# A layer's mixers written as whole helpers with priority between projection units, instead of as interleaved streams of steps

## The chip, the cores and the metric

The kernel runs on one core of one Trainium2 chip. A core has TensorE (PE), VectorE (DVE), ScalarE (ACT), GpSimd (POOL) and SyncE (SP, which issues DMAs here), each with its own in-order queue of instructions, synchronised by semaphores. The metric is device time of one execution in microseconds; the time of a kernel is the median of its runs.

## What is computed

Two consecutive layers of a bidirectional encoder, on x of 2048 tokens by 1024 channels in float32. Each layer modulates its input with a scale and a shift from a conditioning vector, projects it, runs two mixers side by side, projects back and normalises:

```python
for l in range(DEPTH):                       # DEPTH = 2
    shift, scale, gate = jnp.split(mod[:, None, :], 3, axis=-1)
    h = x * (1.0 + scale) + shift
    if l % 2 == 0:  y = even_mixer(h, ...)   # neighbourhood attention || GLA
    else:           y = odd_mixer(h, ...)    # HGRN2 || Mamba-2 SSD
    x = layer_norm(DEEPNORM_ALPHA * x + gate * y, ln_g[l], ln_b[l])
```

The change is in the odd layer. Its mixer splits the projection into columns for HGRN2 (four heads of 128: cq, two forget gates cf_f and cf_b, ci, and the output gate cg) and for the state-space branch (its gate dz, 1024 channels dxbc, and dt). HGRN2 is a gated linear recurrence run in both directions; the state-space branch first filters dxbc along the sequence with four taps and SiLU, and then runs two chunked scans:

```python
oc = bidir_gated_recurrence(qc, bhld(ci, HGRN_HEADS), k_f, lf_f, k_b, lf_b)
yc = rms_norm(oc, hgrn_norm_g) ... * jax.nn.silu(cg)
xbc = lax.conv_general_dilated(dxbc, conv_w[:, None, :], ...)      # 4 taps
xs, bm, cm = split_cols(jax.nn.silu(xbc + conv_b), ...)
y = ssd_chunked(x_fw, a_fw, bm, cm) + rev(ssd_chunked(...)) + d_skip * xs
yd = rms_norm(y * jax.nn.silu(dz), ssm_norm_g)
return jnp.concatenate([yc, yd], axis=-1) @ w_out
```

## The kernel before, in words

**Projection.** A layer's input projection is cut into units (qf0 to qf3, ci0, ci1, b0, b1, x0 to x3, g0, g1, dz0, dz1 in the odd layer). Each unit has a weight that is loaded, split by ScalarE and GpSimd into a high and a low part (`wh`, `wl`, lines 185 and 186), and multiplied with the modulated input in high and low parts (`hH`, `hL`): three matmuls for each of eight slices of 128 channels (line 205). The sequence is done in two halves of 1024 tokens, half 1 first; a half has two groups of 512 tokens, g. `block` computes one tile of a unit and yields after every second slice, so a unit is a generator of steps. A finished tile is evacuated by ScalarE or VectorE and stored to DRAM by a DMA. `turn` is the change of halves: dz0 and dz1 of half 1 mixed with the building of half 0's input.

**HGRN2.** `Rec.pass_a(sg, ...)` (line 465) does one head on one stretch of 512 tokens (sg 0 to 3) in 12 steps: seven levels of a doubling scheme. A level multiplies `Q` and `Kp` by decay products `T` on VectorE (lines 532 and 534; line 536 is a third product on GpSimd), and has 16 small matmuls into a bank named `fine` (line 459), from which VectorE takes entries into `S` (line 497); the last level writes a bank `l` (line 522). Then come transposes `pk` (line 551), state updates `pu` (562) and output products `po` (580, 585). `pass_b` (line 608) is the second direction and the normalisation; `other(h, sg)` runs it for two heads.

**State-space branch.** `Ssd.steps` computes the step sizes and decays of one half, with five `sp` matmuls. `Ssd.conv` filters: a tile is 128 channels (i, 0 to 7) by 512 tokens (sg): load `cvx`, first tap on ScalarE (line 1152), three taps on VectorE (line 1154), sigmoid on ScalarE (1155), product on GpSimd (1156); for i under 6 four transposes `cvt` by TensorE (1165), a copy and a store. `cvx` and `cva` have two buffers. `Ssd.backward` (`back`) does one chunk of 128 tokens of the backward scan: load of `tk`, a GpSimd product (1203), two matmuls `pu` (1211) and the state step `sb` (1219, 1220). `local` and `forward` run later, beside the output projection.

**Order.** The program is not the order on the chip. A list scheduler simulates a time line with its own costs and issues, on each engine, what is ready, taking first what stands first in the program; `tc.high_priority(offset=2000)` counts an instruction as if it stood that much further ahead. In the kernel before, the odd layer's program order is itself fine: `woven(front, streams)` writes the steps of the units one by one, and after given numbers of them one step of a stream. HGRN2's chain (`lagging` mixes two stretches of a head half a pass apart) is one stream, in half 0 with `other` chained behind it; the steps, conv and back are another. A stream is given as (generator, first, per): it starts at front step `first`, and a step of it is written after every `per` front steps. `conv` is pipelined by one tile: `filtered` starts a tile, `put` transposes the one before. The even layer's attention has its own `weave`, which the change leaves.

What the odd layer's half 1 comes to in the program:

```python
woven(chained(steps_of("qf1 ci1 qf2 b1 qf3 x0 x1 x2 x3 g0 g1", 1), turn),
      (hgrn(range(4), 1), 0, 2), (chained(steps(1), conv(3), back(3)), 90, 8))
```

## Time and profile before

| what | value |
|---|---|
| time, median of 3 runs | 2748.59 us (2747.47 to 2750.7) |
| the profiled execution's own time | 2755.94 us |
| its span, first to last instruction | 2754.1 us |
| mean granted TensorE clock | 0.955 |
| busy: PE, DVE, ACT, POOL | 2526.8, 1493.4, 1122.9, 1326.1 us |

The profile is of one execution; its busy times and durations belong to that execution's time, which is not the median. A busy PE can still be slow: the granted clock says by how much, 1.00 being the full 2.4 GHz. The even layer and the beginning of the odd one, up to 1403.0 us of the span, are in both kernels the same instructions in the same order; the stages after it are cut at the first matmuls of ci0 (half 1), dz0 in the turn, ci0 (half 0), g1 (half 0), at the end of the last dz1 matmul, and at the first matmul of the output projection.

### The profile page before, as it was taken

Reading aid. Unit: us, or ns where it says so; the run is one execution under the profiler, and the core shown is the slowest. Engines: PE = TensorE matmul, PEld = TensorE weight load, DVE = VectorE, ACT = ScalarE, POOL = GpSimd, SP = SyncE. Lnnn points to the kernel's source line nnn. Section 1 sums busy time; section 2 is a strip of 40 time slices with the busy share of each in tenths; the row PEclk is TensorE's granted clock in tenths of the full one; section 3 lists DMA queues with packets and bytes.
Section 4 is the critical chain, followed back from the end, with each engine's and each line's share of the span. In section 5 each row is a group of like instructions: output and inputs, shape, how many; then the busy total and the mean of one; then the engine's idle time right before and its main releaser. Section 6 shows DMA issues by size and latency. Waiting matters only on the chain. (4 is left out here: it accounts for less than half of the span.)

```text
span 2754.1 us, 53110 instructions
## 1 busy us (share of the span) xinstructions
PE 2526.8 (92%) x20888; PEld 2125.2 (77%) x20888; DVE 1493.4 (54%) x2493; ACT 1122.9 (41%) x2355; POOL 1326.1 (48%) x1305
## 2 busy tenths in 40 slices
PE   7999999999999799998999999999999888788987
PEld 5877778887778677877788777888877677566776
DVE  6223335124433676765626356432625788687895
ACT  3152323244343644543323444232424453554652
POOL 4252325244442544434535556335534677575874
PEclk9999999999999899999999999999999999798998
DMA  8525434323365878775553335434436567543331
GB/s 275 159 99 169 145 115 132 115 95 106 109 221 181 253 210 234 202 205 167 173 201 126 106 124 177 136 127 131 134 105 207 169 200 235 182 148 112 117 115 62
DMA packets 269800, 432.46 MB, mean 157 GB/s; under 512 B 25936, under 2 KB 143600, under 8 KB 269552
## 3 DMA queue, kind: packets, MB, share of 16 engines
q1 hardware_dynamic: 267248, 420.69, 48.7%
q0 software_dynamic: 2304, 8.39, 0.8%
q8 instruction: 165, 2.70, 0.4%
q14 instruction: 83, 0.68, 0.1%
HBM read 296.60 MB, written 132.38 MB: 156 GB/s over the span
## 5 line engine op out<-in xcount | busy, mean ns | idle before, releaser
L186 POOL TENSOR_TENSOR wl<-wraw,wh 128x1024 fp32r<-128x1024 f32 (+2 forms) x116 | 290.5, 2524 | 293.9 <-ACT wh L185 293.0
L1032 PE MATMUL oo<-wo,yH 128*128 128x512 f32 x1024 | 309.9, 418 | 21.8 <-ACT yH L1003 20.2
L536 POOL TENSOR_TENSOR Kp<-Kp,T 128x256 f32<-128x256 f32 x144 | 125.7, 873 | 275.1 <-ACT F L492 111.7
L1032 PEld LDWEIGHTS oo<-wo,yH 128*128 128x128 f32 x1024 | 199.8, 201 | 65.3 <-ACT yH L1003 23.5
L860 POOL TENSOR_TENSOR nap<-nap,nasm 128x384 f32<-128x384 f32 (+2 forms) x128 | 115.7, 914 | 209.5 <-DVE nasm L859 192.2
L534 DVE TENSOR_TENSOR Kp<-Kp,T 128x256 f32<-128x256 f32 x144 | 103.7, 720 | 146.6 <-PE fine L459 60.2
L185 ACT CAST wh<-wraw 128x1024 fp32r<-128x1024 f32 (+2 forms) x116 | 116.8, 1052 | 154.5 <-PE obqk L205 27.4
L1032 PE MATMUL oo<-wo,yL 128*128 128x512 f32 x512 | 172.4, 405 | 3.0 <-DVE yL L1004 3.0
L532 DVE TENSOR_TENSOR Q<-Q,T 128x512 f32<-128x512 f32 x144 | 146.9, 1020 | 0.0
L885 PE MATMUL nay<-napts,nav 128*128 128x128 f32 (+1 forms) x832 | 121.5, 289 | 20.2 <-ACT napts L872 13.7
L885 PEld LDWEIGHTS nay<-napts,nav 128*128 128x128 f32 (+1 forms) x832 | 114.5, 202 | 31.3 <-ACT napts L872 16.1
L1154 DVE SCALAR_TENSOR_TENSOR cva<-cvx,cw,cva 128x512 f32<-128x512 f32 x96 | 104.2, 1098 | 30.5 <-ACT cva L1152 29.4
L1032 PEld LDWEIGHTS oo<-wo,yL 128*128 128x128 f32 x512 | 97.5, 193 | 23.5 <-DVE yL L1004 4.2
L205 PE MATMUL oqf<-hH,wh 128*128 128x512 f32 x256 | 104.8, 409 | 4.5 <-ACT wh L185 4.5
L205 PE MATMUL ox<-hH,wh 128*128 128x512 f32 x256 | 106.2, 415 | 0.0
L497 DVE COPY_PREDICATED S<-lmask,fine 128x128 f32<-128x128 int32 x160 | 43.7, 297 | 111.3 <-PE fine L459 111.2
L205 PE MATMUL ox<-hH,wl 128*128 128x512 f32 x256 | 102.7, 401 | 0.0
L205 PE MATMUL ox<-hL,wh 128*128 128x512 f32 x256 | 102.5, 400 | 0.0
L205 PE MATMUL oqf<-hL,wh 128*128 128x512 f32 x256 | 102.4, 400 | 0.0
L205 PE MATMUL oqf<-hH,wl 128*128 128x512 f32 x256 | 101.9, 399 | 0.5 <-POOL wl L186 0.5
L858 ACT ACTIVATE nap<-nap,namx 128x384 f32<-128x384 f32 (+2 forms) x128 | 79.2, 619 | 50.6 <-DVE namx L857 50.3
L156 POOL TENSOR_TENSOR hL<-hf,hH 128x512 fp32r<-128x512 f32 x36 | 50.2, 1403 | 96.9 <-ACT hH L155 96.9
(375 smaller groups left out, 7723.8 us busy)
## 6 DMA issues: line engine op xcount, KB each, us to landing
wraw<-in_o_w_dram SPq DMA_DIRECT2D x56, 512.0 KB
wraw<-in_e_w_dram SPq DMA_DIRECT2D x44, 512.0 KB
adw<-in_ada_w_dram SPq DMA_DIRECT2D x32, 512.0 KB
tk<-xtok SPq DMA_DIRECT2D x31, 384.0 KB
nat<-in_na_tab_dram SPq DMA_DIRECT2D x16, 640.0 KB
xt<-in_x_dram SPq DMA_DIRECT2D x16, 512.0 KB
adw<-in_ada_p_dram SPq DMA_DIRECT2D x16, 512.0 KB
naq<-aq SPq DMA_DIRECT2D x64, 128.0 KB
```

The lines of the kernel that those rows point to most:

```text
L156: (nc.vector if d % 2 and not act else nc.gpsimd).tensor_sub(hL[:, d, :], hf, hH[:, d, :].bitcast(F32))
L185: nc.scalar.copy(h[:, sl], raw)
L186: (nc.vector if e.wl_dve else nc.gpsimd).tensor_sub(l[:, sl], raw, h[:, sl].bitcast(F32))
L205: nc.tensor.matmul(oo, a, b, start=d == 0 and m == 0, stop=d == ND - 1 and m == 2)
L532: nc.vector.tensor_tensor(qv, qv, view(tcur, toff + 1, [[nb - 1, 2], [2, n2], [0, s]]), ALU.mult)
L534: nc.vector.tensor_tensor(kv, kv, view(tcur, toff + nb + 1, [[2, n2], [0, s]]), ALU.mult)
L536: nc.gpsimd.tensor_tensor(kv, kv, view(tcur, toff, [[2, n2], [0, s]]), ALU.mult)
L858: nc.scalar.activation(p[:, :nk], p[:, :nk], AF.Exp, bias=mx, scale=-1.0, accum_out=sm)
L860: nc.gpsimd.tensor_tensor(p[:, :nk], p[:, :nk], sm.broadcast_to([P, nk]), ALU.mult)
L885: nc.tensor.matmul(s.yp[:, n, :], b.vs[:kb, n, j, :], s.pts[n][:kb, j, :], start=j == 0, stop=j == nj - 1)
L1032: nc.tensor.matmul(os[n], ops[m][0][:, c, :], ops[m][1][c][:, ns], start=x == 0, stop=x == 23)
L1154: nc.vector.scalar_tensor_tensor(acc, xr[:, k:k + SW], cw[:, i, k:k + 1], acc, ALU.mult, ALU.add)
```

## The change

`woven` is removed. `hgrn`, `conv`, `back`, `steps` and `other` are no longer generators: each call writes the whole helper at once, under `tc.high_priority(offset=2000)`, at one place between two units. HGRN2 takes one head at a time, both stretches one after the other; conv takes one stretch of 512 tokens, without the lag of one tile; the backward scan's two halves (`weighted`, `update`) are one function again. The units of half 0 have another sequence, and the `dtt` tile comes from pool `mp` under the tag `KT` instead of from `kp` under `cvt`. In the output projection `other(2, ...)` gets the same priority. The diff, cut to its core (lines of `yield` that go are left out):

```diff
-def woven(front, *streams):
...
-    def conv(self, pool, bank, sgs, xbc, cw, cb):
+    def conv(self, pool, bank, sg, xbc, cw, cb):
...
-        def filtered(i, sg):
...
+        for i in range(8):
             xr = pool.tile([P, SW + 4], F32, name="cvx", tag="cvx", bufs=e.cv_bufs)
...
-        for i in range(8):
-            for sg in sgs:
-                done.append(filtered(i, sg))
-                if len(done) > 1:
-                    put(*done.pop(0))
-                yield
-        put(*done.pop(0))
...
-            xw = self.weighted(c, 1, tk, pool, tk[:, :512].rearrange("p (h q) -> p h q", h=8))
-            yield
-            pu = self.update(xw, tk[:, 512:], bank)
+            pu = self.update(c, 1, tk, tk[:, 512:], pool, bank, tk[:, :512].rearrange("p (h q) -> p h q", h=8))
...
-    def hgrn(hs, half):
-
-        def chain(sg):
-            for h in hs:
-                yield from recs[h].pass_a(sg, hgrn_prep(e, mp, cq[h], cz[h], lb[:, h:h + 1], ub[:, h:h + 1]),
-                                          v_loader(e, mp, ci[h // 2][:, (h % 2) * P:(h % 2 + 1) * P], P), sg % 2)
-        return lagging(chain(2 * half + 1), chain(2 * half), Rec.STEPS // 2)
+    def hgrn(h, half):
+        for sg in (2 * half + 1, 2 * half):
+            with tc.high_priority(offset=2000):
+                run(recs[h].pass_a(sg, hgrn_prep(e, mp, cq[h], cz[h], lb[:, h:h + 1], ub[:, h:h + 1]),
+                                   v_loader(e, mp, ci[h // 2][:, (h % 2) * P:(h % 2 + 1) * P], P), sg % 2))
 
     sd = Ssd(e, sg_, dz, y[512:1024])
 
-    def conv(*sgs):
-        return sd.conv(kp, xbank, sgs, xbc, cw, cbias)
-
-    def back(*sgs):
-        for sg in sgs:
-            for c in range(4 * sg + 3, 4 * sg - 1, -1):
-                yield from sd.backward(c, kp, xbank)
+    def conv(sg):
+        with tc.high_priority(offset=2000):
+            sd.conv(kp, xbank, sg, xbc, cw, cbias)
+
+    def back(sg):
+        for c in range(4 * sg + 3, 4 * sg - 1, -1):
+            with tc.high_priority(offset=2000):
+                sd.backward(c, kp, xbank)
 
     def steps(half):
-        return sd.steps(sp, kp.tile([P, 4, NC // 2, 16], F32, name="dtt", tag="cvt", bufs=1), xbank, dt_raw, half)
+        with tc.high_priority(offset=2000):
+            sd.steps(sp, mp.tile([P, 4, NC // 2, 16], F32, name="dtt", tag="KT", bufs=1), xbank, dt_raw, half)
 
     def btags(t, par):
         return {"qul": (("F", "Kp")[t], 2), "stwb": ((("stw", "kd"), ("q", "KT"))[t][par], 1), "sq": (f"S32{t}", 1),
...
         return mps.tile([P, 512], F32, name=name, tag="rg" if name == "pob" else "sd", bufs=2)
 
     def other(h, sg, tags=None):
-        return pass_b(e, recs[h:h + 2], sg, mp, bbank, tags or [btags(t, sg % 2) for t in range(2)])
+        with tc.high_priority(offset=2000):
+            run(pass_b(e, recs[h:h + 2], sg, mp, bbank, tags or [btags(t, sg % 2) for t in range(2)]))
 
     w1 = ip.load(U["b0"])
     for g in range(2):
...
     gate = gate_row(e, mp, (("T0", 1), ("T1", 1)), lambda n: mps.tile([P, 512], F32, name=n, tag="rf00", bufs=1), cols1[:, 2 * ND:])
     wout1 = gated_ahead(e, mp, "Q", i["o_w_out"], gate, "1")
     units("ci0", 1)
+    hgrn(0, 1)
+    units("qf1", 1)
+    hgrn(1, 1)
+    units("ci1 qf2 b1", 1)
+    hgrn(2, 1)
+    units("qf3", 1)
+    hgrn(3, 1)
+    units("x0 x1 x2 x3", 1)
     sd.prepare(sp, i["dt_bias"], i["a_log"], i["d_skip"])
-    turn = ip.turn(U["dz0"], U["dz1"], 1, U["qf0"], U["b0"], 0,
-                   lambda n: mp.tile([P, 4, 2 * P], F32, name="xt", tag=f"T{n % 2}", bufs=1), banks(mps, "rg", 2))
-    woven(chained(steps_of("qf1 ci1 qf2 b1 qf3 x0 x1 x2 x3 g0 g1", 1), turn),
-          (hgrn(range(4), 1), 0, 2), (chained(steps(1), conv(3), back(3)), 90, 8))
+    steps(1)
+    conv(3)
+    back(3)
+    units("g0 g1", 1)
+    run(ip.turn(U["dz0"], U["dz1"], 1, U["qf0"], U["b0"], 0, lambda n: mp.tile([P, 4, 2 * P], F32, name="xt", tag=f"T{n % 2}", bufs=1), banks(mps, "rg", 2)))
     units("ci0", 0)
-
-    def last():
-        yield from steps_of("qf1 ci1 g0 qf2 b1 qf3 x0 x1 x2 x3 g1", 0)
-        late = []
-        for nm in ("dz0", "dz1"):
-            late.append((U[nm], ip.load(U[nm])))
-            yield from ip.blocks(*late[-1], 0, 0)
-        for u, w in late:
-            yield from ip.blocks(u, w, 0, 1)
-
-    woven(last(), (chained(hgrn(range(2), 0), *(other(0, sg) for sg in range(4)), hgrn(range(2, 4), 0), other(2, 0)), 0, 2.15),
-          (chained(steps(0), conv(2, 1, 0), back(2, 1, 0)), 122, 2.67))
+    hgrn(0, 0)
+    units("qf1", 0)
+    hgrn(1, 0)
+    units("g0 ci1", 0)
+    steps(0)
+    units("x0 x1 x2 x3", 0)
+    for sg in range(4):
+        other(0, sg)
+    conv(2)
+    back(2)
+    conv(1)
+    units("qf2", 0)
+    back(1)
+    units("b1", 0)
+    conv(0)
+    units("qf3", 0)
+    hgrn(2, 0)
+    hgrn(3, 0)
+    back(0)
+    units("g1", 0)
+    late = []
+    late.append((U["dz0"], ip.load(U["dz0"])))
+    run(ip.blocks(*late[-1], 0, 0))
+    late.append((U["dz1"], ip.load(U["dz1"])))
+    run(ip.blocks(*late[-1], 0, 0))
+    other(2, 0)
+    for u, w in late:
+        run(ip.blocks(u, w, 0, 1))
     closed("pp1", "sp1", "wa1")
     wp = opened("po1", "right")
     obank = banks(opened("pops1", "right", space=PSUM), "oo", 2)
...
         if 0 < c < NC - 1:
             sd.local(c + 1, mp, sbank)
         if c % 4 == 1 and c < 12:
-            run(other(2, c // 4 + 1, ftags))
+            other(2, c // 4 + 1, ftags)
         op.tile(c, (4, 8), c == NC - 1, sd.forward(c, mp, sbank))
     closed("po1", "pops1", "hp1", "hgrn", "hgrnps", "conv", "wb1", "hgrnc", "ssdc")
 
```

Three places of the order that results, for the engines that wait or are waited for. In the changed kernel line numbers are lower (1154 is 1135, 532 is 519, 534 is 521, 497 is 484, 522 is 509, 459 is 446, 396 is 383, 1220 is 1182); `x8` is that many alike in a row.

VectorE where the filter of sg 2 and 1 begins in half 0. `cva` is a filter product, `Q`, `Kp` and `S` belong to HGRN2 levels, `gt` to `other`, `sb` to back, `F` to the start of a pass. Before:

```order
L532 TENSOR_TENSOR Q<-Q,T 128x2x32x8
L1154 SCALAR_TENSOR_TENSOR cva<-cvx,cw,cva 128x512 x6
L497 COPY_PREDICATED S_21590<-lmask,fine 128x128
L532 TENSOR_TENSOR Q<-Q,T 128x2x16x16
L534 TENSOR_TENSOR Kp<-Kp,T 128x8x32
L532 TENSOR_TENSOR Q<-Q,T 128x2x8x32
```

In the changed kernel:

```order
L647 SCALAR_TENSOR_TENSOR gt<-pyb,c_hgrn_g,gt 128x512 x3
L1135 SCALAR_TENSOR_TENSOR cva<-cvx,cw,cva 128x512 x22
L1182 TENSOR_TENSOR sb<-sb,pu 128x512
L1135 SCALAR_TENSOR_TENSOR cva<-cvx,cw,cva 128x512 x2
L1182 TENSOR_TENSOR sb<-sb,pu 128x512 x3
L1135 SCALAR_TENSOR_TENSOR cva<-cvx,cw,cva 128x512 x12
L667 TENSOR_SCALAR F<-F,ub,lb 128x1024
```

The filter's products stood in the gaps of the HGRN2 chains of heads 2 and 3; now they stand in blocks, with only back's states between, and those chains follow.

VectorE further on, beside unit g1 before and beside the dz units in the changed kernel (`st` is a unit's tile on its way out, `KT` a transposed `Kp`). Before:

```order
L375 TENSOR_TENSOR st<-st,og_22184 128x512
L534 TENSOR_TENSOR Kp<-Kp,T 128x64x4
L555 COPY KT<-pk 128x512
L497 COPY_PREDICATED S_22039<-lmask,fine 128x128
L1154 SCALAR_TENSOR_TENSOR cva<-cvx,cw,cva 128x512
L532 TENSOR_TENSOR Q<-Q,T 128x2x128x2
L1154 SCALAR_TENSOR_TENSOR cva<-cvx,cw,cva 128x512 x2
L534 TENSOR_TENSOR Kp<-Kp,T 128x32x8
```

In the changed kernel:

```order
L519 TENSOR_TENSOR Q<-Q,F 128x2x256
L521 TENSOR_TENSOR Kp<-Kp,T 128x4x64
L519 TENSOR_TENSOR Q<-Q,T 128x2x4x64
L521 TENSOR_TENSOR Kp<-Kp,T 128x128x2
L1182 TENSOR_TENSOR sb<-sb,pu 128x512
L521 TENSOR_TENSOR Kp<-Kp,T 128x64x4
L484 COPY_PREDICATED S_22588<-lmask,fine 128x128
L519 TENSOR_TENSOR Q<-Q,T 128x2x128x2
L383 TENSOR_TENSOR st<-st,odz_23436 128x256
L542 COPY KT<-pk 128x512
L521 TENSOR_TENSOR Kp<-Kp,T 128x32x8
```

Between the same kinds of HGRN2 instructions there are no filter products any more.

TensorE at the end of half 0's units: `odz` are the last matmuls of dz1, `pcb` belongs to the first SSD chunk of the output projection's stage. Before:

```order
L205 MATMUL odz_23609<-wh,hH 128x256
L522 MATMUL l_23579<-Q,Kp 64x64 x8
L205 MATMUL odz_23609<-wl,hH 128x256
L205 MATMUL odz_23609<-wh,hL 128x256
L1238 MATMUL pcb<-bc 128x128 x2
L551 MATMUL pk<-c_ident,Kp 128x128 x8
L562 MATMUL pu<-v,KT 128x128 x8
L580 MATMUL po<-v,Sf 128x128 x4
```

In the changed kernel:

```order
L446 MATMUL fine<-Q,km 32x32 x16
L205 MATMUL odz_23732<-wh,hH 128x256
L205 MATMUL odz_23732<-wl,hH 128x256
L205 MATMUL odz_23732<-wh,hL 128x256
L446 MATMUL fine<-Q,Kp 32x32 x16
L1200 MATMUL pcb<-bc 128x128 x2
L509 MATMUL l_23002<-Q,Kp 64x64 x8
L538 MATMUL pk<-c_ident,Kp 128x128 x8
L549 MATMUL pu<-v,KT 128x128 x8
L567 MATMUL po<-v,Sf 128x128 x4
```

Of the last HGRN2 pass only the `l` level stood among the last `odz` rows; now two `fine` levels and `l` stand there and behind them.

## Rows read from the trace of the kernel before

**Rows 1.** The page: span; busy time of the engines; one group: busy, mean ns.

```profile
span 2754.1 us, 53110 instructions
...
PE 2526.8 (92%) x20888; PEld 2125.2 (77%) x20888; DVE 1493.4 (54%) x2493; ACT 1122.9 (41%) x2355; POOL 1326.1 (48%) x1305
...
L1154 DVE SCALAR_TENSOR_TENSOR cva<-cvx,cw,cva 128x512 f32<-128x512 f32 x96 | 104.2, 1098 | 30.5 <-ACT cva L1152 29.4
```

**Rows 2.** Windows of six stages: length, busy time (instructions) of each engine, clock, DMA.

```profile
1403.00:1758.00 355.00, 346.42 (x3453) 284.31 (x3452) 192.84 (x285) 143.60 (x247) 182.68 (x195) 0.99 0.45 147
1758.00:1867.20 109.20, 109.20 (x826) 99.53 (x825) 36.34 (x59) 32.29 (x59) 39.92 (x29) 1.00 0.45 143
1867.20:2196.90 329.70, 315.32 (x2772) 261.17 (x2771) 161.09 (x259) 131.53 (x267) 160.77 (x172) 0.98 0.46 148
2196.90:2332.60 135.70, 117.76 (x1365) 102.40 (x1365) 115.45 (x158) 63.78 (x124) 104.19 (x97) 0.96 0.66 214
2332.60:2393.20 60.60, 37.84 (x175) 30.74 (x175) 42.88 (x78) 36.40 (x109) 33.77 (x31) 0.71 0.62 216
2393.20:2754.10 360.90, 310.80 (x1448) 255.08 (x1448) 281.66 (x406) 172.41 (x482) 228.73 (x233) 0.92 0.34 110
```

**Rows 3.** PE's waits, 1403:1867.2: line waited for, us in total, times, longest.

```profile
PE oci L205 <- DVE dt_raw L1588: 4.3, 1, 4.3
```

**Rows 4.** PE's waits in the window 1867.2:2196.9.

```profile
PE cvt L1165 <- POOL cva L1156: 5.3, 4, 2.3
PE sp L1126 <- ACT edkf L1128: 4.6, 1, 4.6
```

**Rows 5.** PE's waits in the window 2196.9:2332.6.

```profile
PE odz L205 <- DVE st L396: 7.0, 4, 3.9
PE cvt L1165 <- POOL cva L1156: 2.9, 2, 1.7
PE l L522 <- DVE Q L532: 2.6, 2, 2.3
...
PE po L585 <- DVE stw L603: 1.6, 1, 1.6
```

**Rows 6.** DVE by line, 2196.9:2332.6: busy us, mean ns | idle before, releasers.

```profile
L1154 DVE SCALAR_TENSOR_TENSOR cva<-cvx,cw,cva 128x512 f32<-128x512 f32 x41 | 42.1, 1041 | 8.6 <-ACT cva L1152 8.3
L532 DVE TENSOR_TENSOR Q<-Q,T 128x512 f32<-128x512 f32 x18 | 19.3, 1073 | 0.0
L534 DVE TENSOR_TENSOR Kp<-Kp,T 128x256 f32<-128x256 f32 x18 | 13.7, 759 | 3.8 <-PE fine L459 1.4 <-ACT F L492 1.3 <-PE l L522 0.7
L1220 DVE TENSOR_TENSOR sb<-sb,pu 128x512 f32<-128x512 f32 x11 | 7.5, 677 | 2.7 <-PE pu L1211 1.6 <-POOL sb L1219 0.6 <-issue 0.5
...
L497 DVE COPY_PREDICATED S<-lmask,fine 128x128 f32<-128x128 int32 x15 | 4.4, 292 | 2.4 <-PE fine L459 2.4
```

**Rows 7.** Windows in which PE runs dense: 512 columns, then 256.

```profile
1380.00:1390.00 10.00, 10.00 (x46) 8.27 (x45) 0.00 (x0) 1.01 (x2) 0.00 (x0) 1.00 0.22 80
...
1806.00:1812.00 6.00, 6.00 (x54) 6.00 (x53) 2.12 (x5) 3.64 (x6) 3.69 (x3) 1.00 0.42 135
```

**Rows 8.** Tile cvx, whole span: duration ns min/median/max, first and last start.

```profile
L1154 DVE SCALAR_TENSOR_TENSOR cva<-cvx,cw,cva x96: 735/752/2897, 1609.7 to 2312.3; 128x512 f32<-128x512 f32 x96
...
L1152 ACT ACTIVATE cva<-cvx,cbias,cw x32: 807/816/825, 1608.6 to 2305.6; 128x512 f32<-128x512 f32 x32
L1155 ACT ACTIVATE cvx<-cva x32: 618/632/643, 1616.3 to 2313.9; 128x512 f32<-128x512 f32 x32
L1156 POOL TENSOR_TENSOR cva<-cva,cvx x32: 1263/1459/1823, 1621.1 to 2314.6; 128x512 f32<-128x512 f32 x32
```

**Rows 9.** Tile cvx in 1631.5:1648, one load and the operation after it.

```profile
L1150 SPq DMA_DIRECT2D cvx<-xbc x1: 319/319/319, 1636.7 to 1636.7; - x1
L1152 ACT ACTIVATE cva<-cvx,cbias,cw x1: 817/817/817, 1639.2 to 1639.2; 128x512 f32<-128x512 f32 x1
```

**Rows 10.** Windows, the instructions of tile cvt alone.

```profile
2131.00:2261.00 130.00, 12.03 (x72) 7.94 (x72) 9.86 (x17) 0.97 0.56 171
```

More of the change, by code (lines that the diff above doesn't have):

```diff
@@ L319, in chained @@
         yield from g
-def woven(front, *streams):
-    due = [first for _, first, _ in streams]
-    for j, _ in enumerate(front):
-        for x, (g, _, per) in enumerate(streams):
-            while due[x] <= j:
-                due[x] += per
-                next(g, None)
-    for g, _, _ in streams:
-        run(g)
 def weave(back, n, k, front):
@@ L1133, in steps @@
         nc.scalar.activation(self.tot[:, hs].rearrange("p c h -> p (c h)"), pt[:, :n * 16], AF.Exp)
-        yield
-    def conv(self, pool, bank, sgs, xbc, cw, cb):
+    def conv(self, pool, bank, sg, xbc, cw, cb):
         e, nc = self.e, self.e.nc
-        done = []
-        def filtered(i, sg):
-            t0 = sg * SW
-            lo, hi = max(t0 - 2, 0), min(t0 + SW + 1, S)
+        t0 = sg * SW
+        lo, hi = max(t0 - 2, 0), min(t0 + SW + 1, S)
+        for i in range(8):
             xr = pool.tile([P, SW + 4], F32, name="cvx", tag="cvx", bufs=e.cv_bufs)
@@ L1156, in filtered @@
             nc.gpsimd.tensor_tensor(acc, acc, xr[:, 0:SW], ALU.mult)
-            return i, t0, acc
-        def put(i, t0, acc):
             if i >= 4:
@@ L1169, in put @@
                                   tt.rearrange("p (c n) -> p c n", c=SC))
-        for i in range(8):
-            for sg in sgs:
-                done.append(filtered(i, sg))
-                if len(done) > 1:
-                    put(*done.pop(0))
-                yield
-        put(*done.pop(0))
-        yield
     def backward(self, c, pool, bank):
@@ L1189, in backward @@
             nc.sync.dma_start(tk, self.tok[c * P:(c + 1) * P, :])
-            xw = self.weighted(c, 1, tk, pool, tk[:, :512].rearrange("p (h q) -> p h q", h=8))
-            yield
-            pu = self.update(xw, tk[:, 512:], bank)
+            pu = self.update(c, 1, tk, tk[:, 512:], pool, bank, tk[:, :512].rearrange("p (h q) -> p h q", h=8))
             new = pool.tile([P, 512], F32, name="sb", tag="sb", bufs=2)
@@ L1195, in backward, with update @@
             self.sb = new
-        yield
-    def weighted(self, c, d, x, pool, xw=None):
+    def update(self, c, d, x, b, pool, bank, xw=None):
         nc = self.e.nc
@@ L1204, in weighted @@
                                 ed[:, c, :].unsqueeze(2).broadcast_to([P, 8, 64]), ALU.mult)
-        return xw
-    def update(self, xw, b, bank):
-        nc = self.e.nc
         pu = bank("pu")
@@ L1287, in forward @@
         if c < NC - 1:
-            pu = self.update(self.weighted(c, 0, tk, pool), tk[:, 512:], bank)
+            pu = self.update(c, 0, tk, tk[:, 512:], pool, bank)
             new = pool.tile([P, 512], F32, name="sf", tag=f"{'kq'[c % 2]}m0", bufs=1)
```

## The prediction

> **What bounds the kernel now.** I read the page first. TensorE (PE) is busy 92% of the span, and no other engine comes to 55% [rows 1]: time goes where PE idles or where its clock is down. The change touches the odd layer alone, and the order of instructions is the same row by row up to the first projection of ci0 in the second half, which the trace starts at 1403.0 us; so nothing before that is in the sum. Next I cut the rest into stages by their first PE instructions [rows 2]: 1403.0 to 1758.0 (units of half 1, HGRN2 chains beside them), to 1867.2 (the "turn": dz0 and dz1 beside the next half's modulated input), to 2196.9 (half 0 as far as g1), to 2332.6 (g1 and the dz units, with what is left of conv, back and the HGRN2 chains of heads 2 and 3), to 2393.2 (junction: no unit is left), and the out-projection. PE idles 8.6, 0, 14.4, 17.9, 22.8 and 50.1 us in them. The stretch before the junction is the weak one: 13% idle with VectorE (DVE) busy 115 of 136 us, against 4% and 161 of 330 in the stage ahead of it. Last I asked what PE waited for, stage by stage [rows 3 to 5]. In the weak stretch it is DVE: odz waits for a result tile to be evacuated (7.0), the level steps l and po wait for DVE products (2.6 and 1.6), and GpSimd (POOL) holds up the convolution's transposes (2.9).
>
> **The change, part by part.** The units' matmuls are the same, in half 0 in another sequence; so are the counts of conv, back, HGRN2 and SSD instructions. What moves is where the helpers stand between the units. I go by stage. The profiled execution took 2755.94 us on a span of 2754.1; it stands 7.35 above the median of the runs (2748.59), and I bring the sum down by that at the end. One unit matmul of 512 columns costs 10.00/46 = 0.217 us where PE runs dense, one of the dz units (256 columns) 6.00/54 = 0.111 [rows 7].
>
> Half 1 and the turn. Before, the steps of the state-space branch, conv(3) and back(3) began while the x units ran; now they are issued after x3, and the order puts 18 of the 24 DVE products of conv(3) into the turn. The turn is dense (109.2 of 109.2 busy) and DVE has 36 of its 109 us in use [rows 2], so the 18 products, 18 x 1.10 = 19.8 us [rows 1], lie beside PE work. Two things are exposed. First, a tile of conv goes load, ScalarE, three DVE products, sigmoid, POOL, four transposes; with two buffers one pair of tiles takes one such cycle. The load took 1639.2 - 1636.7 = 2.5 us [rows 9]; then 0.82 + 3 x 0.75 + 0.63 + 1.46 by the medians [rows 8], and four transposes at 12.03/72 = 0.67 [rows 10]: 8.3 us, or 9.4 with DVE products at their mean of 1.10 [rows 1]. In the order 69 to 71 dz matmuls stand between pairs, 7.8 us, with the pair's own transposes 9.1. The excess of 0.3 comes twice: +0.6. Secondly, the three groups of sp matmuls of the steps now stand 21 and 24 rows apart, where before one of the two gaps was 460; the one wait like it took 4.6 us [rows 4], and some 21 dz matmuls (2.3 us) cover half of that: +2.3. Together **+3**. Below, all 8.6 us of idleness in the stage go (the largest named one, 4.3, is an oci behind a DVE copy [rows 3]); above, +20: both sp gaps cost their 4.6 and conv's two gaps take the 14.4 us of rival B.
>
> Half 0 as far as g1. The steps and the whole of conv(2) and conv(1) now run while no HGRN2 chain does, since those of heads 2 and 3 come after qf3. Between pairs stand 42 to 48 unit matmuls, 9.1 to 10.4 us, with the transposes 10.4 to 11.7, over the cycle of 8.3 to 9.4. So the 5.3 us of cvt waits [rows 4] would go, and the bunched sp matmuls cost about as much: the 4.6 there is once more than once. I take **0**; the ends are -14.4 (all idleness) and rival B.
>
> The weak stretch. The order has fewer DVE instructions between the evacuations of the first g1 tile and the last dz1 tile: 18 conv products for 36, 6 sb for 11, against 25 Q for 22, 22 Kp for 21 and 17 S for 14. At the means of the stretch [rows 6] these five kinds come to 18.7 + 4.1 + 26.8 + 16.7 + 5.0 = 71.3 us now and 37.5 + 7.4 + 23.6 + 15.9 + 4.1 = 88.5 before: DVE has 17 us less to do in 136. Its waits of 7.0 + 2.6 + 1.6 = 11.2 [rows 5] are queueing behind just these products; I let half go (-5.6) and a quarter of the 2.9 behind POOL (-0.7). The granted clock there is 0.96, against 0.98 in the stage before [rows 2]; with a third of the idle time gone I bring it to 0.98: 117.8 x 0.02 = -2.4. Together **-9**; the ends are 0 and -22 (rival A).
>
> The junction. At the end of the units the order shows one level of the last HGRN2 pass left before, and three steps now (two fine levels and l), with three dz matmuls and a pcb between them. A level that nothing covers is its fine matmuls, then S and Q behind each other in DVE's queue (0.29 and 1.07 [rows 6]), then the next level's matmuls; I take 2.2 us, of which 0.8 is my estimate for matmuls and signals: two more are **+4.5**. Below, other(2), which now has priority, covers them: 0. Above, +7, with Kp (0.76) in both chains and the clock of 0.71 that this stage already has [rows 2].
>
> The out-projection has the same first row, and small exchanges after it (pyb and pin by a few rows); its operands come as before: 0. Two of 56 activation-table loads go, on ScalarE, which PE hardly waits for here: 0. The dtt tile takes its space from KT rather than the transposes' copy: steps(1) then waits for a KT copy of the last HGRN2 pass, which lies ahead of it anyway: 0.
>
> Sum: +3 + 0 - 9 + 4.5 = -1.5, or 2754.4 for an execution like the profiled one, **2747 us** on the median's basis. A measurement of this kernel can tell about 0.2%, 5.5 us, from no change; so the forecast is none that can be told, with 2736 to 2757 as its own range.
>
> **The rivals.** A, faster: the weak stretch loses its pattern altogether. For it: DVE is the only engine there that is near full (115 of 136 us), and 17 us are taken from it. Against: odz's wait is four times and 3.9 us at the longest, which is one long product and not a full queue, and the chains of heads 2 and 3 now run nearly whole beside that stretch. Price: the 17.9 us idle there, 117.8 x 0.03 = 3.5 for a clock of 0.99, and 5.3 of the cvt waits: -26.7, which gives 2722.
>
> B, slower: conv becomes the pacemaker. PE takes its queue in order, so a transpose whose tile isn't filtered holds up the unit matmuls behind it, and through them the evacuations and the next weights. Between 2131 and 2261 us the transposes came at 130.0/18 = 7.2 us a tile, 14.4 a pair [rows 10]. Were that the pace of conv itself and not of the HGRN2 chains beside it, six gaps in half 0 would cost 14.4 - 10.4 = 4.0 each and two in the turn 14.4 - 9.1 = 5.3, together 34.6, of which 8.2 (5.3 and 2.9 of cvt waits [rows 4, 5]) are in the span already: +26, or 2775. It decides from a cycle of 10.4 us on. For it: one DVE product took 2.90 us where the median is 0.75 [rows 8], so the three products can take 3 to 9 us, and a block of 22 products is all that DVE's queue now holds in one place. Against: with no chain beside it the cycle adds up to 8.3 to 9.4.
> On that lengthening there is a rule: the Trainium skill, "SBUF — State Buffer", section "SBUF: two separate sides", says that the port pair which DVE and GpSimd share is an exclusive lock held for a whole instruction, and that the other side blocks. The trace agrees in kind (0.74 to 2.90 us for one shape). By the rule each buffer's products meet the other buffer's POOL product (1.46) once a cycle, which gives an estimated 10.8 us in place of 9.4; six gaps at 0.4 and two at 1.7 would add 6 to the sum where the rows add 0.6.
>
> That the change does nothing is excluded by the order, which moves conv by some hundreds of rows.
>
> **How the numbers follow.** The forecast gets 0.46, A 0.24, B 0.30: B a little ahead of A, since whole blocks with priority give the in-order queues long runs of one kind, while what A needs is 17 us of room in one stretch only. Of the forecast's 0.46, 0.26 lie within 0.2%, 0.12 under (the -9 nearer to its end) and 0.08 over. That makes 0.36 faster, 0.26 same and 0.38 slower. The range runs from 2720, just past A, to 2787, which takes in B with a third gap in each conv of half 0 (3 x 4.0).
>
> **What would show it.** Cut at the same PE instructions, half 1 with the turn should take 467 us (464 before), half 0 to g1 330, the weak stretch 127 with odz waits under 4 us, the junction 65. Rival A shows as a weak stretch under 120. Rival B shows as cvt waits of 4 us behind POOL or DVE, two for each conv, and a stage to g1 over 345. The forecast is wrong if the idle time sits elsewhere: if the units wait for weights (wh, wl) since ScalarE or POOL are taken by a block with priority, or if the out-projection waits for back's last states.

## The result, and the profile after

The changed kernel takes 2720.55 us (median of 4 runs, 2718.31 to 2730.57) against 2749.64 for the kernel before beside it: a ratio of 0.9898, with a 95% interval of 0.9868 to 0.9927. It is faster by 1%, where the forecast was none that can be told (2747). The range of 2720 to 2787 holds it by half a microsecond, and that is luck: the lower end was set by rival A, and neither A's reason nor that of the likeliest case is what happened.

The page of the changed kernel, first lines:

```profile
span 2717.4 us, 53129 instructions
...
PE 2504.4 (92%) x20888; PEld 2110.3 (78%) x20888; DVE 1469.5 (54%) x2493; ACT 1121.1 (41%) x2353; POOL 1317.8 (48%) x1305
```

The profiled execution took 2719.21 us, near its median, while that of before stood 7 above its own. So of the 36.7 us between the two spans some 7 belong to the executions. The six stages (length, busy time of PE, PEld, DVE, ACT and POOL, granted clock, DMA):

```profile
1397.90:1757.50 359.60, 353.42 (x3591) 292.21 (x3590) 178.81 (x279) 131.09 (x231) 166.65 (x188) 0.99 0.42 138
1757.50:1870.40 112.90, 106.92 (x688) 96.24 (x687) 46.95 (x64) 45.93 (x75) 48.38 (x35) 0.98 0.52 162
1870.40:2195.70 325.30, 314.31 (x2635) 262.40 (x2634) 167.68 (x265) 134.51 (x269) 171.04 (x169) 0.99 0.53 170
2195.70:2321.60 125.90, 115.19 (x1469) 100.98 (x1467) 99.76 (x149) 58.85 (x116) 86.90 (x97) 0.95 0.58 189
2321.60:2378.70 57.10, 36.86 (x205) 30.47 (x205) 43.23 (x82) 37.60 (x113) 33.58 (x34) 0.73 0.56 195
2378.70:2717.40 338.70, 301.63 (x1448) 245.25 (x1448) 275.02 (x406) 171.29 (x482) 236.48 (x234) 0.96 0.37 118
```

Against [rows 2]: up to 1403.0 us, where nothing in the order differs, 5.1 less, which is the executions' own; half 1 with the turn 472.5 (464.2 before), half 0 up to g1 325.3 (329.7), the weak stretch 125.9 (135.7), the junction 57.1 (60.6), and the out-projection 338.7 in place of 360.9. One cut of [rows 2] lies 1 us too early: the last dz1 matmul of the kernel before ends at 2333.6, as the cuts were meant, and there the weak stretch and the junction of before are

```profile
2196.90:2333.60 136.70, 118.76 (x1383) 103.33 (x1382) 115.81 (x160) 64.10 (x125) 104.39 (x98) 0.96 0.66 213
2333.60:2393.20 59.60, 36.84 (x158) 29.81 (x156) 42.52 (x78) 36.09 (x109) 33.56 (x31) 0.70 0.63 219
```

so that the weak stretch lost 10.8 and the junction 2.5 us. The largest single gain, 22 us, is in the stage that I had put down as unchanged. PE's waits, of the weak stretch and then of half 1 with the turn (line waited for, us in total, times, longest):

```profile
PE fine L446 <- DVE Q L519: 3.8, 2, 3.2
PE po L567 <- ACT uo L553: 3.7, 1, 3.7
PE odz L205 <- DVE st L383: 2.0, 3, 0.8
```

```profile
PE odz L205 <- DVE st L383: 4.4, 4, 3.4
...
PE sp L1117 <- ACT edkb L1113: 1.1, 1, 1.1
```

The waits for the evacuations of dz have left the weak stretch (7.0 before [rows 5], 2.0 now) and stand in the turn (none before, 4.4 now). Its longest is 3.4 us; the evacuation that ends it stands on DVE behind three filter products and one product of the next half's input, 4.8 us together, while ScalarE's part of it had started at 1792.2:

```profile
1790.76 3.09 DVE L1135 SCALAR_TENSOR_TENSOR cva<-cvx,cw,cva 128x512 f32<-128x512 f32 x3 [0.77 <-ACT cva L1133]
1793.77 1.75 DVE L156 TENSOR_TENSOR hL<-hf,hH 128x512 fp32r<-128x512 f32 x1
1795.44 0.41 DVE L383 TENSOR_TENSOR st<-st,odz 128x256 f32<-128x256 f32 x1
```

The cvt waits have nearly gone (the line of half 0 up to g1, where [rows 4] has 5.3):

```profile
PE cvt L1143 <- POOL cva L1137: 0.8, 2, 0.4
```

Where did the out-projection lose its time before? The window around its first pass of `other(2, ...)` in the kernel before, and PE's waits in it:

```profile
2465.20:2489.20 24.00, 12.72 (x44) 9.98 (x44) 21.45 (x35) 13.59 (x48) 15.89 (x20) 0.72 0.37 127
```

```profile
PE pd L1250 <- ACT E L1253: 4.3, 1, 4.3
PE pcb L1238 <- DVE syo L1302: 4.1, 1, 4.1
PE pt L1300 <- ACT yacc L1297: 2.8, 1, 2.8
```

PE idles 11.3 of 24 us, and the clock falls to 0.72 with it, while DVE is busy for 21.45. Of what DVE does there, its largest group and the product that PE waits for:

```profile
L1257 DVE SCALAR_TENSOR_TENSOR w<-c_t_ge,dt,w 128x128 f32<-128x128 f32 x13 | 10.7, 873 | 0.0
...
L1302 DVE TENSOR_TENSOR syo<-pt,c_ssm_g 128x512 f32<-128x512 f32 x1 | 0.7, 683 | 0.0
```

Thirteen `w` products of later chunks are ahead of `syo` in DVE's queue, and PE's queue has the next chunk's `pcb` behind that: 4.1 of the 11.3 us. The 4.3 before `pd` lead back to such products too, by way of ScalarE: its E stood behind `ti`, `ti` waited 3.5 us for DVE's `yacc`, and ahead of that stood five `w`:

```profile
2463.62 4.21 DVE L1257 SCALAR_TENSOR_TENSOR w<-c_t_ge,dt,w 128x128 f32<-128x128 f32 x5
2467.76 1.52 DVE L1292 TENSOR_TENSOR yacc<-yacc,dzl 128x512 f32<-128x512 f32 x1
2469.31 0.63 ACT L1294 ACTIVATE ti<-yacc 128x512 f32<-128x512 f32 x1 [3.52 <-DVE yacc L1292]
```

The 2.8 before `pt` are for ScalarE, whose own queue has sixteen products of later chunks ahead of that `yacc`. The counts of instructions are the same in both kernels' stages, 1448 on PE and 406 on DVE: this is a matter of the order of the queues, not of work.

### The profile page after: what moved, and what is told of

Its sections match the earlier page's. It is cut to its first block, busy times and chain, and to the rows that moved or that the text cites. A ratio compares the mean times of both kernels' runs of the same rounds, so it can differ in the third digit from the quotient of the medians.

```text
span 2717.4 us, 53129 instructions
## 1 busy us (share of the span) xinstructions
PE 2504.4 (92%) x20888; PEld 2110.3 (78%) x20888; DVE 1469.5 (54%) x2493; ACT 1121.1 (41%) x2353; POOL 1317.8 (48%) x1305
## 4 chain that ended last, share of the span: by engine, by line
PE 56%; DMA 15%; DVE 12%; ACT 5%; issue 5%; POOL 4%; SPq 3%; POOLq 0%; DVEq 0%; ACTq 0%
PE oo L1019 7%; PE ox L205 5%; PE oqf L205 5%; PE obv L205 4%; PE og L205 3%; DMA adw<-in_ada_w_dram 3%; PE oag L205 3%; PE fine L446 3%; PE oci L205 3%; PE oav L205 3%; PE oak L205 2%; PE obg L205 2%; DMA nak<-ak 2%; DVE w L1219 2%; PE odz L205 2%
## 5 line engine op out<-in xcount | busy, mean ns | idle before, releaser
L1019 PE MATMUL oo<-wo,yH 128*128 128x512 f32 x1024 | 300.3, 407 | 21.2 <-ACT yH L990 19.0
L1019 PEld LDWEIGHTS oo<-wo,yH 128*128 128x128 f32 x1024 | 193.4, 194 | 63.9 <-ACT yH L990 24.9
L523 POOL TENSOR_TENSOR Kp<-Kp,T 128x256 f32<-128x256 f32 x144 | 118.0, 820 | 235.3 <-PE l L509 71.1
L519 DVE TENSOR_TENSOR Q<-Q,T 128x512 f32<-128x512 f32 x144 | 138.3, 961 | 0.0
L1135 DVE SCALAR_TENSOR_TENSOR cva<-cvx,cw,cva 128x512 f32<-128x512 f32 x96 | 95.8, 1010 | 58.6 <-ACT cva L1133 57.2
L1019 PEld LDWEIGHTS oo<-wo,yL 128*128 128x128 f32 x512 | 96.1, 191 | 23.6 <-DVE yL L991 4.9
L61 DVE SCALAR_TENSOR_TENSOR acc<-adw,csil,acc 128x1024 f32<-128x1024 f32 x28 | 41.1, 1468 | 105.7 <-DMA adw<-in_ada_w_dram 105.7
```

The lines of the kernel that those rows point to most:

```text
L519: nc.vector.tensor_tensor(qv, qv, view(tcur, toff + 1, [[nb - 1, 2], [2, n2], [0, s]]), ALU.mult)
L523: nc.gpsimd.tensor_tensor(kv, kv, view(tcur, toff, [[2, n2], [0, s]]), ALU.mult)
L1019: nc.tensor.matmul(os[n], ops[m][0][:, c, :], ops[m][1][c][:, ns], start=x == 0, stop=x == 23)
L1135: nc.vector.scalar_tensor_tensor(acc, xr[:, k:k + SW], cw[:, i, k:k + 1], acc, ALU.mult, ALU.add)
```

## The experiments

Twelve kernels ran, each beside the kernel before. Half 1 and half 0 of either kernel can be put together freely, since the units and helpers have the same data; the priority in the out-projection's loop is a third piece, the dtt tile a fourth.

**First: which piece.** Four kernels. In these kernels `other` and the rest are the generators of before, and the whole helpers with priority have a W at their names. e1_outplain is the changed kernel, written with these helpers, with `run(other(2, c // 4 + 1, ftags))` in the out-projection's loop as before, without the priority.

> The changed kernel, with the four calls of other(2, ...) that stand in the out-projection's loop written without the priority (there are three such calls; everything ahead of the out-projection is in the same order). Theory 1: the priority of these calls is what took 22 us out of the out-projection in the profiles (360.9 to 338.7 us), so this kernel loses it: 2735 to 2743 us, an out-projection stage over 350 us. Rival: the stage's gain came from elsewhere or varies from run to run: 2718 to 2724 us, the stage at 337 to 343.

e2_outprio puts the priority on that line of the kernel before, and only there:

```diff
         if c % 4 == 1 and c < 12:
-            run(other(2, c // 4 + 1, ftags))
+            otherW(2, c // 4 + 1, ftags)
```

> The kernel before, with the priority put on the calls of other(2, ...) in the out-projection's loop and nothing else. Theory 1: it takes the out-projection's gain alone: 2727 to 2736 us. Rival (the gain is not from this priority): 2746 to 2752 us, the stage at 355 or more.

e3_half1new and e4_half0new take one half from each kernel, without the priority in the loop. e3's difference from the kernel before:

```diff
-    woven(chained(steps_of("qf1 ci1 qf2 b1 qf3 x0 x1 x2 x3 g0 g1", 1), turn),
-          (hgrn(range(4), 1), 0, 2), (chained(steps(1), conv(3), back(3)), 90, 8))
+    hgrnW(0, 1)
+    units("qf1", 1)
...
+    stepsW(1)
+    convW(3)
+    backW(3)
+    units("g0 g1", 1)
...
```

> Half 1 with its turn as in the changed kernel, half 0 and the out-projection as before. In the profiles half 1 and turn went from 464.2 to 472.5 us, so theory: 2755 to 2759 us (the new half 1 costs 8). Rival: the 8 us are the difference of two executions and half 1 is worth nothing: 2747 to 2752 us.

> Half 1 with its turn and the out-projection as before, half 0 as in the changed kernel. In the profiles half 0 with the junction went from 526.0 to 508.3 us (-17.7). Theory: 2731 to 2735 us. If the new half 0 also decides how the out-projection starts: 2710 to 2720 us. If the gain is the out-projection's alone: 2745 to 2750 us.

Measured: e1 2729.57 us (ratio 0.9929, 0.9911 to 0.9947), e2 2761.65 (1.0034, 1.0020 to 1.0048), e3 2743.16 (0.9970, 0.9956 to 0.9984), e4 2716.32 (0.9876, 0.9857 to 0.9895). The new half 0 brings the whole gain, the out-projection's part with it, and the new half 1 takes some of it back (e1 and e4 differ by half 1 alone). The priority in the loop, my first theory for the out-projection, falls: e1 is without it and its stage takes 345.4 us, not over 350 (its time lies between the two expectations); on the kernel before it makes the stage longer (368.2), and e2 is slower than even its rival said. And e3, whose program from half 0 on is that of the kernel before, has an out-projection of 343.0 us:

```profile
2396.80:2739.80 343.00, 303.90 (x1448) 247.20 (x1448) 275.87 (x406) 172.11 (x482) 233.24 (x234) 0.95 0.37 117
```

The orders explain it: the last 1000 TensorE instructions of e1, e3 and e4 are the same, one by one, and differ from those of before. Though nothing in e3's out-projection was edited, the scheduler issued it in another order, presumably since it came to it at another moment of its simulated time.

**Second: is it the order alone?** e11_dtt makes one small edit of the change to the kernel before, which has no bearing on the out-projection:

```diff
-        return sd.steps(sp, kp.tile([P, 4, NC // 2, 16], F32, name="dtt", tag="cvt", bufs=1), xbank, dt_raw, half)
+        return sd.steps(sp, mp.tile([P, 4, NC // 2, 16], F32, name="dtt", tag="KT", bufs=1), xbank, dt_raw, half)
```

> The kernel before with one edit of the change alone: the dtt tile from pool mp under the tag KT. By the order its last 1000 TensorE instructions are those of the kernels whose out-projection took 342 to 345 us, and not those of the kernel before (361). Theory: the out-projection's time hangs on which of a few orders the scheduler falls into, and any small edit ahead of it can choose: a stage of 341 to 346 us and 2730 to 2737 us in all, with the weak stretch still at 134 to 140. Rival: the order is not what makes the 16 us, the whole helpers are: stage 355 or more, 2745 to 2752 us.

Measured 2739.92 us (0.9953, 0.9936 to 0.9971). Its stages of half 0 up to g1, weak stretch, junction and out-projection:

```profile
1867.40:2195.50 328.10, 312.62 (x2820) 258.52 (x2818) 164.53 (x262) 130.92 (x267) 165.61 (x174) 0.99 0.47 148
2195.50:2333.10 137.60, 120.82 (x1322) 106.41 (x1319) 116.13 (x155) 64.06 (x123) 100.93 (x96) 0.93 0.67 210
2333.10:2394.50 61.40, 36.45 (x174) 28.35 (x172) 42.22 (x78) 36.80 (x109) 31.72 (x30) 0.75 0.61 211
2394.50:2737.80 343.30, 303.88 (x1448) 247.14 (x1448) 275.42 (x406) 172.15 (x482) 232.25 (x234) 0.95 0.36 117
```

Half 0 is as slow as before, and the out-projection takes 343.3 us, as expected from its order. (The time is 3 us over what was expected; its half 1 with the turn takes 468.8, 4.6 more than before.) So some 18 us of the gain are the out-projection's order, which a change of no consequence chooses as well. (By the medians e11 is 12.3 us under the kernel before: about the 17.6 of this stage less 4.6 in half 1 with the turn and 1.1 in half 0 with the junction.) In the table stages are grouped by that order.

| kernel | half 1 + turn | half 0 + junction | out-projection | its order | median, us |
|---|---|---|---|---|---|
| before | 464.2 | 526.0 | 360.9 | D | 2749.6 |
| after | 472.5 | 508.3 | 338.7 | A | 2720.6 |
| e1_outplain | 472.2 | 510.8 | 345.4 | B | 2729.6 |
| e2_outprio | 464.6 | 521.0 | 368.2 | own | 2761.7 |
| e3_half1new | 472.1 | 525.9 | 343.0 | B | 2743.2 |
| e4_half0new | 461.3 | 508.8 | 344.7 | B | 2716.3 |
| e5_h0new_prio | 462.6 | 510.1 | 340.5 | A | 2718.2 |
| e6_convnoprio | 464.5 | 511.6 | 358.9 | own | 2739.4 |
| e7_noprio | 464.1 | 520.9 | 360.5 | C | 2747.5 |
| e8_hgrnnoprio | 465.0 | 512.7 | 362.1 | C | 2737.2 |
| e9_h1hgrn | 466.7 | 501.7 | 342.0 | B | 2714.3 |
| e10_best | 466.5 | 507.8 | 345.4 | own | 2718.9 |
| e11_dtt | 468.8 | 527.1 | 343.3 | B | 2739.9 |
| e15_moredve | 463.9 | 514.9 | 358.3 | D | 2743.1 |

(Stages are of one profiled execution each, medians of all runs; kernels with one letter share the last 1000 TensorE instructions. "Own" orders differ from one another.) With A the stage takes 338.7 and 340.5 us, with B 342.0 to 345.4 in five kernels, with C 360.5 and 362.1, with D 360.9 and 358.3: e15, with other code ahead of it, fell into the order of the kernel before and has its time. One count parts the good orders from the bad, that of the `w` products which stand on DVE between a chunk's `yacc` (line 1292) and its `syo` (line 1302; numbers of the kernel before), summed over all chunks: 0 in B, 3 in A and 11 in e10, with 338.7 to 345.4 us; 22 in D, 26 in C and e6 and 42 in e2, with 358.3 to 368.2. No run moved these products alone, so that they are the cause is argued and not shown.

The table also tells how far two executions of one order lie apart. In half 0 and the junction TensorE has the same instructions in the same order in before and e3 (526.0 and 525.9), in after and e1 (508.3 and 510.8), in e4 and e5 (508.8 and 510.1) and in e9 and e10 (501.7 and 507.8); and e2, which leaves the order of before only in the junction, takes 521.0. In half 1 the order of before takes 461.3 to 465.0 in eight kernels. A difference of 5 or 6 us in half 0 is thus not clear of this spread.

**Third: what helps in half 0.** Two kernels on e4's base take priorities away, a third all of them:

```diff
     def convW(sg):
-        with tc.high_priority(offset=2000):
+        if True:
```

> New half 0 on the old half 1 (the kernel of 2716 us), with the priority taken from conv and back in half 0; HGRN2, other and steps keep it. In its order 18 filter products, in place of 13, stand in the middle of the last 120 VectorE instructions of the units. Theory 1 (the gain in the weak stretch is VectorE freed of filter products): the weak stretch rises from 126 to 130 to 136 us and the time to 2720 to 2727. Rival (the gain is HGRN2's priority): 2714 to 2719, the stretch at 125 to 128.

> New half 0 on the old half 1, whole helpers in the same places, and no priority at all. In its order 42 filter products stand in the last 140 VectorE instructions of the units (21 with priority), and 26 more VectorE instructions come after the units. Theory: the place alone does not help, priority is what brings HGRN2 forward; the weak stretch is at 134 or over and the junction over 65, 2735 to 2755 us. Rival (the place between the units is what counts): 2714 to 2722.

> New half 0 on the old half 1 (2716 us with all its priorities), with the priority taken from HGRN2's passes and other in half 0; conv, back and steps keep it. The end of its order is that of the kernel without any priority (2747 us). Theory: with conv alone ahead, HGRN2 is left over at the end of the units: junction over 68 us, 2738 to 2752 us. Rival (conv and back were what needed it): 2714 to 2725 us, junction under 60.

Measured: e6 2739.37 us (0.9953, 0.9937 to 0.9968), e7 2747.46 (0.9984, 0.9964 to 1.0004), e8 2737.24 (0.9948, 0.9929 to 0.9967). The medians mislead here, since all three fell into orders of the out-projection that take 359 to 362 us; the stages tell more. The weak stretch of e6, and the weak stretch and junction of e7:

```profile
2184.10:2321.50 137.40, 117.89 (x1539) 104.55 (x1538) 113.97 (x162) 67.12 (x133) 99.79 (x108) 0.95 0.65 202
```

```profile
2173.50:2306.50 133.00, 115.10 (x1361) 99.43 (x1359) 111.44 (x149) 63.22 (x120) 97.26 (x97) 0.95 0.58 180
2306.50:2381.80 75.30, 45.80 (x381) 37.09 (x379) 62.15 (x111) 44.49 (x132) 45.52 (x45) 0.77 0.67 231
```

Without conv's priority 36 filter products are in the weak stretch again (41 before [rows 6], 23 in e4). PE's waits for DVE are back there, 11.5 us (5.3 in e4):

```profile
PE fine L459 <- DVE Q L532: 4.8, 5, 1.6
...
PE l L522 <- DVE Kp L534: 1.4, 1, 1.4
PE odz L205 <- DVE st L396: 1.3, 1, 1.3
...
PE l L522 <- DVE Q L532: 1.2, 2, 0.8
```

```profile
L1195 DVE SCALAR_TENSOR_TENSOR cva<-cvx,cw,cva 128x512 f32<-128x512 f32 x36 | 37.9, 1054 | 8.1 <-ACT cva L1193 7.9
```

and the stretch at 137.4 us; yet half 0 with its junction is only 2.8 us longer than e4's, since the stage up to g1 got shorter (320.4 for 327.5). Without HGRN2's priority the remainder comes after the units: the junction takes 75.3 us in e7 and 68.9 in e8. With no priority at all half 0 takes 520.9, 5 less than before and as much as e2's 521.0, so that the places alone are not shown to gain anything; with one of the two priorities it takes 512, with both 508.8 and 510.1. So most of the gain of 17 us needs a priority, either of the two will do (`steps` kept its own with both), and what the second adds is within the spread. (e7 is within theory's time, with a weak stretch of 133.0 for the 134 expected, e8 1 us under it; e6 is 12 us over theory 1, by its out-projection.)

e15_moredve puts DVE work back into the weak stretch of e4 and edits nothing else:

```diff
-                    nc.vector.copy_predicated(S32[:, hi], e.lmask[:, lev, :].unsqueeze(1).broadcast_to([P, SC, 32]),
-                                              pt[hi])
+                    for _ in range(1 + getattr(self, "more", 0)):
+                        nc.vector.copy_predicated(S32[:, hi], e.lmask[:, lev, :].unsqueeze(1).broadcast_to([P, SC, 32]),
+                                                  pt[hi])
...
     def hgrnW(h, half):
+        recs[h].more = 4 if h > 1 and half == 0 else 0
```

> New half 0 on the old half 1 (2716 us), with the masked copy into S done five times over in place of once in the fine levels of heads 2 and 3 in half 0 (the output is unchanged): 80 more VectorE instructions of 0.295 us, of which the order puts some 50, 15 us, into the weak stretch; nothing else moves there. Theory 1 (it is VectorE's time in the stretch that the change freed, 17 us of filter products for 11 us of stretch): the weak stretch goes from 126 back to 134 to 139 us, with fine, l and odz waiting for VectorE. Rival (what helped is that HGRN2 stands ahead, VectorE has room): 129 us or less. The whole time also hangs on the out-projection, whose order is another one than the kernel of 2716 us has, so the stage decides, not the whole.

Measured 2743.06 us (0.9977, 0.9964 to 0.9991), with the order D of the out-projection (358.3). Its weak stretch and junction, and the masked copies in the stretch:

```profile
2195.40:2321.20 125.80, 112.33 (x1447) 97.31 (x1449) 107.91 (x208) 54.15 (x105) 83.67 (x96) 0.99 0.55 180
2321.20:2382.40 61.20, 37.29 (x237) 30.48 (x237) 49.58 (x97) 40.42 (x122) 33.58 (x35) 0.72 0.60 201
```

```profile
L498 DVE COPY_PREDICATED S<-lmask,fine 128x128 f32<-128x128 int32 x89 | 26.4, 297 | 5.3 <-PE fine L459 4.2
```

The theory's stage did not come: 70 of the 80 copies are in it, DVE is busy 107.9 us there (96.1 in e4; seven `w` products moved out), and the stretch is as long as in e4. The junction is 5.9 us longer: HGRN2's end came later. So 80 copies of 0.297, 23.8 us of DVE work, cost 5 or 6 us of half 0 by e4 and e5, no more than its spread. By that price, a quarter of itself, the 17 us of filter products that left the stretch would explain 4 or 5 of the 17 us gained. That is an estimate: the copies stand elsewhere in DVE's queue than the filter products did. What makes up the rest is not shown.

**Fourth: half 1.** In e9_h1hgrn HGRN2 stays as in the changed kernel and steps, conv(3) and back(3) run as a stream again:

```diff
     hgrnW(3, 1)
-    units("x0 x1 x2 x3", 1)
...
-    stepsW(1)
-    convW(3)
-    backW(3)
-    units("g0 g1", 1)
...
+    woven(chained(steps_of("x0 x1 x2 x3 g0 g1", 1), turn), (chained(steps(1), conv(3), back(3)), 6, 8))
```

> New half 0, and in half 1 only HGRN2 as wholes with priority, while steps, conv(3) and back(3) run as a stream of steps beside the x units, as before, so that no filter work stands in the turn. Theory: the 8 to 11 us that the new half 1 costs are steps and conv in the turn, where odz waits for VectorE (4.4 us) and the clock drops: half 1 with turn 460 to 464 us, 2714 to 2719. Rival (whole HGRN2 passes cost it): 470 or more, 2724 to 2730.

Measured 2714.26 us (0.9880, 0.9854 to 0.9906). Half 1 with the turn takes 466.7 us (466.5 in e10), between the two expectations: conv and steps in the turn cost 5.5 of the 7 to 11 us by which e1 (472.2) lies over the eight kernels with the old half 1 (461.3 to 465.0). What is left for the whole passes, 2 to 5 us, is hardly clear of the spread.

**Last: the pieces put together.** e5 and e10 add the priority in the loop to e4 and e9:

> Half 1 as before, half 0 as in the changed kernel, and the priority on other(2, ...) in the out-projection, as in the changed kernel. Theory: the stages add, since each has its own order: half 1 with turn 461 us (472 in the changed kernel), half 0 and junction 508, the out-projection 339 with the priority where it was 345 without: 2708 to 2713 us, 5 below the kernel with the new half 0 alone (2716). Rival: the priority's worth hangs on how the stage starts (it cost 12 us on the kernel before), here too: 2716 to 2730.

> The kernel with the new half 0, HGRN2 as wholes in half 1 and steps, conv and back as a stream there (2714 us), with the priority on other(2, ...) in the out-projection added. Its order of the out-projection is one that no kernel here has had. Theory (the priority is good for 3 to 6 us there when half 0 is the new one): 2708 to 2713 us. Rival (another order, another time): 2714 to 2735 us.

Measured: e5 2718.18 us (0.9882, 0.9858 to 0.9905), e10 2718.93 (0.9877, 0.9850 to 0.9903). Neither theory's 5 us came in the medians, though e5's out-projection took 340.5 us for e4's 344.7. e4, e5, e9 and e10 have overlapping intervals; by the median e9 is the fastest, by the ratio to the kernel before beside it e4, both 1.2% under it. Their intervals overlap with the changed kernel's too, so that e4 or e9 beats it by 4 to 6 us is likely and not shown.

## Why the prediction came out as it did

**The step that failed is "The out-projection ...: 0".** I read "the same first row, and small exchanges after it" as the same work in nearly the same order. The exchanges were worth more than all other terms together: -22.2 us between the two profiles. Of that, 13 us are idle time of PE (50.1 before [rows 2], 37.1 after) and 9 are PE's busy time at a higher clock (0.92 and 0.96). e3 and e11 show that it is the order and not the priority, which was the only edit in that stage: they run the loop of before in 343.0 and 343.3 us. I had the exchanges before me and did not cost them: in the one window shown above, `w` products ahead of `syo` and of `yacc` stand behind 8.4 of 11.3 us of idle PE.

**Half 1 and the turn: +3, measured +8.3.** The sign was right; the two costs named were not the ones. sp waited 1.1 us for the 2.3 I took, and cvt next to nothing. Instead the dz units' evacuations queue behind the filter products on DVE (odz, 4.4 us, most of it the one wait shown above), and the turn, dense before, idles 6.0. I had written that 19.8 us of DVE work "lie beside PE work"; but in an in-order queue the evacuations stand behind it, and PE waits for these.

**Half 0 up to g1: 0, measured -4.4.** The cvt waits went (5.3 to 0.8) and sp cost 1.1 where it had cost 4.6, so the blocks of conv did keep up with the units, as the cycle of 8.3 to 9.4 us against 10.4 to 11.7 said. A unit's wait of 3.4 us for a ScalarE evacuation (oqf) is new. A good part of the 4.4 us can be spread: after and e1, in one order, took 325.3 and 328.0.

**The weak stretch: -9, measured -10.8 (-9.8 on the cut of [rows 2]).** DVE's waits went from 11.2 to 6.2 us, the half that I let go, and the cvt wait is gone. The number was nearly right, and the mechanism in part: e6 brings filter products, DVE waits and the 137 us back together, but in e15 more DVE work there leaves the stretch as long as it was and lengthens the junction, and in e6 what the stretch loses is gained in the stage ahead of it. The stretch is no unit of account; half 0 with its junction is.

**The junction: +4.5, measured -2.5 (-3.5 on the cut of [rows 2]).** The two more levels are there, but I added them to a chain that had slack. Before, PE waited there mostly for ScalarE (E, uo and yH, 16.5 us):

```profile
PE pd L1250 <- ACT E L1253: 7.1, 3, 3.6
PE po L580 <- ACT uo L566: 5.2, 1, 5.2
PE oo L1032 <- ACT yH L1003: 4.2, 1, 4.2
```

It seems that these waits run down while the levels go on; no run tried that alone. The wait for uo now stands ahead of the cut, in the weak stretch (3.7). The rows of the changed kernel's junction have a smaller E and a new wait behind DVE:

```profile
PE pd L1212 <- ACT E L1215: 3.9, 1, 3.9
PE oo L1019 <- ACT yH L990: 3.8, 1, 3.8
PE py L1235 <- DVE w L1222: 3.1, 1, 3.1
```

**Rival B** (conv as pacemaker) did not come; half 0 up to g1 got shorter. The lengthening on which it rested is still there, and no worse: the filter product's row after the change has the same spread as in [rows 8].

```profile
L1135 DVE SCALAR_TENSOR_TENSOR cva<-cvx,cw,cva x96: 736/752/2915, 1610.1 to 2259.3; 128x512 f32<-128x512 f32 x96
```

The rule that DVE and GpSimd lock each other out for whole instructions (the Trainium skill, "SBUF — State Buffer", section "SBUF: two separate sides") would, as I used it, have had conv's own products collide more in blocks; their mean went down instead, from 1.098 [rows 1] to 1.010 us:

```profile
L1135 DVE SCALAR_TENSOR_TENSOR cva<-cvx,cw,cva 128x512 f32<-128x512 f32 x96 | 95.8, 1010 | 58.6 <-ACT cva L1133 57.2
```

The trace thus has lengthened products and doesn't show that blocks make more of them.

**Rival A** gave 2722, 1.5 us from the median, and is not what happened: it wanted the 17.9 us of the weak stretch gone, and 10.7 us of idleness are still there after the change. It met the number by way of another stage.

## What to carry to other kernels

Where a scheduler writes the order, cost every stage whose order differs, also those whose program was not edited; compare the orders and look for what stands ahead of an operand that the bounding engine waits for. Before crediting an edit with a gain, look whether an edit of no consequence finds the same order: here one tile's pool was worth 18 us in a stage that never sees it, and 12 us of the whole time. Know first how far two executions of one order lie apart, stage by stage: here by up to 6 us. When work is moved beside a dense stage, ask which evacuations stand behind it in that engine's queue, and count neighbouring stages together.

## What was not expected of the hardware

Little, beside the spread of single executions: the layer ahead of the change, the same instructions in the same order, took 1395.4 to 1403.6 us in the fourteen profiles. A window with much idleness of PE carries a lower granted clock: 0.72 of the full 2.4 GHz where PE was busy for 12.7 of 24 us. At the same distance from the stage's start e11, where PE was busy for 22.1 of 24 us, has 1.00:

```profile
2466.50:2490.50 24.00, 22.08 (x117) 18.34 (x115) 21.80 (x34) 16.17 (x51) 16.75 (x19) 1.00 0.41 137
```

In the out-projection 13 us less of idle time came with 9 us less of busy time for the same 1448 matmuls, so that there the idle time weighed more than itself; some of the 9 can be the difference of the two executions, whose common part up to 1403 us had 13 us less of busy time too (1289.5 and 1276.1).
